# A decoder block with product-key experts on one core: six un-normed query units, six score banks, an earlier decode and a first phase of 88 blocks

## The chip, the core and the metric

The kernel runs on one core of a Trainium2 chip. The metric is the device time of one execution in microseconds (us). The engines are TensorE (PE, with its weight loads PEld), VectorE (DVE), ScalarE (ACT), GpSimd (POOL) and SyncE (SP, which issues DMAs).

## What is computed

One layer on 512 tokens of width 1024, in fp32. Its first half mixes gated linear attention and sliding-window attention. The second half is PEER: each of 8 heads finds, for each token, the 16 best of 16384 experts by two sets of 128 keys, and sums the chosen experts. Cut to what matters here:

```python
h = rmsnorm(x, norm_mix_g); proj = h @ w_in               # GLA and attention branches follow
x = x + (sigmoid(gate_a) * y_a + sigmoid(gate_b) * y_b) @ w_out
xn = rmsnorm(x, norm_ffn_g)
qp = (xn @ w_pq).reshape(t, 8, 2, 128)                    # 16 query units of 128
scores = einsum('thpd,hpkd->thpk', qp, sub_keys)          # 128 keys a side
s_top, i_top = top_k(scores, 16)
cand = s_top[:, :, 0, :, None] + s_top[:, :, 1, None, :]  # 16 x 16, the best 16 of them
best, pos = top_k(cand, 16)
idx = i_top0 * 128 + i_top1                               # at pos
gate = softmax(best)
out = sum_k gate_k * gelu(expert_u[idx_k] . xn) * expert_v[idx_k]
x = x + out
```

## The kernel before

**Precision and weights.** Each fp32 weight unit (128 x 1024) is loaded (raw), cast to fp32r by ACT (whi, line 162) and completed by a subtraction on DVE or POOL (wlo, line 172). A product takes three matmuls: hi by hi, hi by lo, lo by hi (`proj`, line 231; a unit of 128 columns takes 24). The splits run ahead of use through three buffers of each kind, so that a late wlo delays TensorE only after about two units.

**Stages in order.** The mixing half runs to 529.8 us. The gate of the linear attention (`gr`) gets a tanh and a product (`gr_act`, `gr_late`) beside the sliding-window attention, whose products are the matmuls of line 489 on the tile pc.

Then 16 query units (wpq). For unit hp, `proj` makes the queries in PSUM. The first NXU units use the un-normed xuh/xul (x times the norm's weight) and DVE multiplies the result by rb, the reciprocal rms of each token; the others use xh/xl, the normed input, which `xn_hi` and `xn_lo` make (rb itself is ready only after the first unit). `scores(hp)` multiplies queries and keys into a PSUM bank (tag PT or O in turn), `top16` finds the best 16 of 128 on DVE, twice eight, and after two units (one head) `cands` does the same with the head's 72 candidates. `xtok_fill` transposes the normed input of the first tokens back to rows (16 transposes) through the same banks PT and O.

Then all 16384 experts are computed densely for tokens 144 to 511, in 128 blocks of 128: a U block (`h_step`, 24 matmuls into hp, gelu on ACT into ring or hw) and a V block (`v_step`, 24 matmuls into the eight accumulators oacc/oa). They run in three phases: U blocks 0 to N0 - 1, then their V blocks, then the same for the next 20 blocks and for the rest. U results that don't fit the ring go to DRAM (hw to hs, on ACT's queue) and come back during V.

**Beside the first phase** runs the route. The generator `route` decodes positions into expert numbers on DVE, in steps; the table RS says behind which block each step stands. A decoded token group is written into the gate table g by 128 scatters (`scatter`, POOL, line 1143, address tile addr) and by one-hot matmuls (`gmm`, gp). LEAD is the block from which `feed` builds the latter. POOLLO is the number of dense units whose wlo POOL makes. For the first 144 tokens, expert rows are fetched instead (`gather`, POOL, line 1310, 26 early "row" and then "rows" in pairs), with a product and an addition on DVE and a gelu of one column on ACT (lines 1281 and 1282) for each.

**The turns.** Ahead of V, `g_load` brings a slice of the gate table (gt); `w_a` multiplies it by the ring (wr) and casts it (wh), `w_b` makes the rest (wl). Behind V, `sum_phase` copies the accumulators out to yT, so that the next U blocks can use the banks; `pump` issues the next step of the row work where a planner's counters (pe, dve, dma, pool) say that there is room. Each engine runs its instructions in the order in which the code issues them; each DMA queue does as well.

Of the kernel before, what the change touches and what calls it, by code (L numbers as in the profile page):

```python
# [20 lines left out]
D = 1024  # L21
T = 512
NT = 4
# [9 lines left out]
NGA = 6  # L33
NXU = 3
RS = (4, 7, 8, 10, 11, 11, 12, 12, 13, 13, 14, 14, 15, 15, 16, 16, 17, 17, 18, 18, 19, 19, 20, 20, 21, 21, 22, 22)
DVELO = 20
NWARM = 11
POOLLO = 8
DS = (1, 3, 5, 7, 9, 11, 13, 16)
# [7 lines left out]
NB = 128  # L47
N0 = 92
NRP = 10
NOO = 4  # L50
AHEAD = 3
LEAD = 23
TAIL = 5
# [30 lines left out]
def tile_block(ctx, tc, xT, wst, smalls, wgk2, keysT, uT, vv, uv_rows, out):  # L84
# [186 lines left out]
    for kb in range(KB):  # L271
        g = S("gmix")[:, kb:kb + 1]
        nc.scalar.activation(hhi[:, kb], xt[:, kb], AF.Copy, scale=g)
        nc.vector.scalar_tensor_tensor(hlo[:, kb], xt[:, kb], g, hhi[:, kb].bitcast(F32), OP.mult, OP.subtract)
        if kb < 4:
            st.first(kb // 2, kb % 2)
    xs = Bt[:, 0]
    rb = F.tile([128, T], F32, name="rb", tag="rb")
# [332 lines left out]
    for d in range(8):  # L611
        w = unit("gr")
        if d == NR:
            flush()
            gb = F.tile([128, KB, T], F32, name="gb", tag="gb")
            side.append(swa())
            nm[0] = 3
            st.defer = True
        ps = proj(w, H, each=tick)
        nc.vector.tensor_tensor(gr[:, d], ps, rb, OP.mult)  # L620
        gr_late()
        if d >= NR:
            gr_act(d)
            if d < 2 * NR:
                gr_act(d - NR)
    for d in range(8):
# [245 lines left out]
    xtok = XP.tile([128, D], F32, name="xtok")  # L872
    xtk2 = XP.tile([128, D], F32, name="xtk2", tag="xtk2")
    x2d = DR.tile([XP_, D], F32, name="x2d")
    x1s = DR.tile([128, NT, D], F32, name="x1s")
# [47 lines left out]
    nc.scalar.activation(rb, rb, AF.Exp, scale=-0.5)  # L923
    newton(rb, ssq, 1.0 / D, xtok[:, T:])
    nc.scalar.copy(x1t[:, :, 7 * 128:], p)
    nc.sync.dma_start(x1s, x1t)
    xn0 = F.tile([128, KB, 256], F32, name="xn0", tag="gr")
    XN, XU = (xh, xl), (xuh, xul)
    misc = XP.tile([128, 512], F32, name="misc")
    qpt = [xtk2[:, 0:T], xtk2[:, T:], misc[:, 0:T]]  # L930
# [8 lines left out]
    def xn_lo(kb):  # L939
        eng = nc.vector if kb in (1, 3, 6) else nc.gpsimd  # L940
        eng.tensor_tensor(xl[:, kb], hr[kb], xh[:, kb].bitcast(F32), OP.subtract)
        h = hr.pop(kb)
        nc.scalar.copy(xn0[:, kb, 0:128], h[:, 0:128])
        nc.scalar.copy(xn0[:, kb, 128:128 + XP_].rearrange("p (r t) -> p r t", t=XG),
                       h[:, None, 128:TG].to_broadcast([128, XR, XG]))

    def xtok_fill(dst, c, n, hf):
        p = PS.tile([128, 512], F32, name="tp", tag="PT" if hf else "O")
        for i in range(4):
            nc.tensor.transpose(p[0:n, i * 128:(i + 1) * 128], xn0[:, hf * 4 + i, c:c + n], ident)  # L950
        nc.scalar.copy(dst[0:n, hf * 512:(hf + 1) * 512], p[0:n, :])


    vt, it, w1, w2 = slot(name="vals"), slot(U32, "idx"), slot(name="w1"), slot(name="w2")
    vals, idx = [[x[:, i * 512:(i + 1) * 512].rearrange("p (t h k) -> p t h k", t=NT, h=8) for i in range(2)] for x in (vt, it)]
# [5 lines left out]
    def top16(jobs):  # L961
# [8 lines left out]
        for v, ix, src, tmp in jobs:  # L970
            nc.vector.max_index(ix[:, 8:16], v[:, 8:16], tmp)

    def scores(hp):
        qp = qps.pop(hp)
        sc = PS.tile([128, NT, 128], F32, name="sc", tag="PT" if hp % 2 else "O")
        for t in range(NT):
# [15 lines left out]
    for hp in range(17):  # L992
        if hp < 16:
            w = unit("wpq")
            ps = proj(w, XU if hp < NXU else XN)
            if hp == 0:
                xn_hi(0)
            if hp < NXU:
                nc.vector.tensor_tensor(qpt[hp], ps, rb, OP.mult)
            else:  # L1000
                nc.scalar.copy(qpt[hp % 2], ps)
            qps[hp] = qpt[hp if hp < NXU else hp % 2]
            if hp == 0:
                for kb in range(1, KB):
                    xn_hi(kb)
                    xn_lo(kb - 1)
                xn_lo(KB - 1)
        if hp:
            scores(hp - 1)
        if hp % 2 and hp >= 3:  # L1010
            cands((hp - 3) // 2)
        if hp == NXU - 1:
# [5 lines left out]
            R = sR.enter_context(tc.tile_pool(name="route", bufs=1, side="left"))  # L1018
            gate = R.tile([128, NT, 8, 16], F32, name="gate")
            best = gate  # L1020
            idf = R.tile([128, NT, 2, 16, 8], BF, name="idf")
# [178 lines left out]
    def route():  # L1200
# [5 lines left out]
        nc.vector.tensor_tensor(idd[:, :, 1:16], idf[:, :, 0, 1:16], idf[:, :, 0, 0:15], OP.subtract)  # L1206
        yield
        mx = R.tile([128, 32], F32, name="gmax")
        nc.vector.tensor_copy(mx, b32[:, :, 0])
# [58 lines left out]

    late, early, used, acc2 = [False], [0], [-1], []
    nxt, born, end, en = [], {}, [False], [0]  # L1270
    sel = XP.tile([128, XG], F32, name="sel")
# [15 lines left out]
    def gather():  # L1287
# [8 lines left out]
        def issue(k):  # L1296
            nonlocal grp, n
            while n < min(n_, k + (3 if late[0] else 2) + 2 * end[0]):
                for i in range(min(2 if late[0] else 1, n_ - n)):
# [50 lines left out]
        issue(0)  # L1350
        pu, pv = 0, 0
        nxt[:] = [0]
        yield
# [21 lines left out]
    def h_step(b, each=None):  # L1375
        w = get("U", b)
        if b < N0 and b % 2 == 0:
            if b % 4 == 0:
                two[0] = PS.tile([128, 2, 512], F32, name="hp2", tag="S2")
            bank = two[0][:, b % 4 // 2]  # L1380
        else:
            bank = PS.tile([128, 512], F32, name="hp", tag=f"M{(b // 2 if b < N0 else b) % 2}")
        ps = proj(w, XN, n=TD, c0=TG, bank=bank, each=each)
# [94 lines left out]
    def pump():  # L1478
        for x in (dve, dma, pool):
            x[0] = max(x[0], pe[0] - SLACK)  # L1480
        for _ in range(2):
            if side and max(dve[0], dma[0], pool[0] - (0 if late[0] else POOLQ)) < pe[0] + SLACK:
                if nxt and not late[0] and pe[0] < born[nxt[0]] + LAND:
# [42 lines left out]

    BANKS = ("S2", "S2", "PT", "O", "M2", "M3", "M0", "M1")
    b_s = NB
    for ph, (b0, b1) in enumerate(PHASES):
        for b in range(b0, b1):  # L1530
            if b == b1 - 1:
                w_a(b0 // 2)
                w_b(b0 // 2)
                w_a(b0 // 2 + 1)
            h_step(b, feed if LEAD <= b < N0 - GL else None)
            if b == RS[0]:
                dve[0] = 27.0
            for _ in range(RS.count(b)):
                next(r_)
            if b == RS[-1]:  # L1540
                side.append(gather())
            if b == N0 - TAIL - 4:
                late[0] = True
            if b == N0 - TAIL - 1:
# [5 lines left out]
            if b == N0 - GL:  # L1550
# [3 lines left out]
                g_load(0, nc.gpsimd)  # L1554
                g_load(1, nc.gpsimd)
            pool[0] = max(pool[0], pe[0] - SLACK)
            if scs:
# [14 lines left out]
        for b in range(b0, b1 - 2 if last else b1):  # L1572
# [8 lines left out]
            if b % 2 == 0 and p + 1 < b1 // 2:  # L1581
                w_b(p + 1)
            v_step(b, b == b0, b == b1 - 1)
            pump()
            if b == NB - 6:
# [3 lines left out]
                nc.sync.dma_start(xr[:, 2:4], x1s[:, 2:4])  # L1589
        if not last:  # L1590
            sum_phase(ph)
    wl_ = [get("V", NB - 2), get("V", NB - 1)]
# [91 lines left out]
```

## Time and profile before

| | |
|---|---|
| runs | 1754.71, 1765.33, 1756.65 us; median 1756.65 |
| profiled execution | 1764.95 us, of which the span is 1763.0 |
| TensorE granted clock, mean | 0.992 |
| busiest engines | PE 98%, DVE 74%, ACT 43%, POOL 40% |
| DMA | 423.88 MB, 240 GB/s in the mean |

The trace is of one execution. A time of a row is from the span's start. Matmul ends are modelled and overlap, so times of neighbouring starts give the pace.

### The profile page before, as it was taken

The page shows a single profiled execution, that of the slowest core. Times are in us where ns is not written, and L with a number is a line of the kernel's source. Part 1 is how long each engine was busy: PE and PEld are TensorE (multiplying, and loading weights), DVE is VectorE, ACT ScalarE, POOL GpSimd, SP SyncE. Part 2 cuts the span into 40 slices and gives each one's busy share as a digit, 9 for nine tenths or more (in the row PEclk, how much of TensorE's full clock was granted, in tenths as well). Part 3 has the DMA queues.
Part 4 walks back from the last instruction along what each step waited for, and adds up shares of the span by engine and source line. Part 5 has one row for each costly group of instructions (what it writes and reads, how often), then busy time and mean ns, then how long its engine had stood idle before and what let it go on. Part 6 is the DMA issues. An engine that isn't in the chain of part 4 may idle for free.

```text
span 1763.0 us, 26377 instructions
## 1 busy us (share of the span) xinstructions
PE 1724.8 (98%) x9866; PEld 1599.9 (91%) x9866; DVE 1304.9 (74%) x2547; ACT 765.9 (43%) x1334; POOL 705.9 (40%) x447
## 2 busy tenths in 40 slices
PE   9999999999998999999999999999999998999998
PEld 7776688988886889999999989999999998999998
DVE  7767624346337996977778746999889998899874
ACT  5545523335244234355555533444444434444441
POOL 0004444445544451778788872222122223233200
PEclk9999999999998999999999999999999999999999
DMA  4214522222234234699999998999999999999963
GB/s 171 96 60 120 166 98 84 84 72 83 90 129 152 79 104 142 137 267 248 278 290 301 294 304 328 412 412 407 408 404 398 371 386 349 401 377 388 378 244 107
DMA packets 163231, 423.88 MB, mean 240 GB/s; under 512 B 34704, under 2 KB 80144, under 8 KB 144288
## 3 DMA queue, kind: packets, MB, share of 16 engines
q1 hardware_dynamic: 118432, 256.06, 41.9%
q0 software_dynamic: 39488, 152.59, 24.3%
q10 hardware_dynamic: 5184, 13.57, 2.1%
q8 instruction: 77, 1.26, 0.3%
q14 instruction: 50, 0.41, 0.1%
HBM read 379.67 MB, written 42.47 MB: 239 GB/s over the span
## 4 chain that ended last, share of the span: by engine, by line
PE 73%; DMA 8%; DVE 7%; POOL 6%; issue 4%; ACT 2%; SPq 0%; DVEq 0%; POOLq 0%; ACTq 0%
PE oa L1445 21%; PE mm L231 18%; PE hp L231 15%; PE oacc L1445 7%; PE mm L248 6%; POOL g L1143 5%; DMA g<-w,addr 2%; DMA rows<-in_uv_rows_dram,misc 2%; DMA row<-in_uv_rows_dram,misc 2%; DMA gt<-g 1%; POOL row L1310 1%; PE sc L977 1%; PE gp L1188 1%; DVE stt L456 1%; DMA raw<-in_uT_dram 1%
## 5 line engine op out<-in xcount | busy, mean ns | idle before, releaser
L162 ACT CAST whi<-raw 128x1024 fp32r<-128x1024 f32 x347 | 361.6, 1045 | 134.9 <-PE mm L231 26.7
L172 DVE TENSOR_TENSOR wlo<-raw,whi 128x1024 fp32r<-128x1024 f32 x266 | 324.4, 1220 | 58.7 <-ACT whi L162 18.8
L231 PE MATMUL hp<-xh,whi 128*128 128x368 f32 x1024 | 345.1, 337 | 10.2 <-ACT hw L1393 5.7
L1310 POOL DMA_INDIRECT rows<-in_uv_rows_dram,misc x118 | 163.5, 1385 | 454.8 <-DVE accv L1342 381.1
L231 PE MATMUL hp<-xh,wlo 128*128 128x368 f32 x1024 | 339.4, 331 | 0.8 <-DVE wlo L172 0.8
L231 PE MATMUL hp<-xl,whi 128*128 128x368 f32 x1024 | 338.8, 331 | 0.0
L1143 POOL DMA_INDIRECT g<-w,addr x128 | 247.4, 1933 | 95.3 <-issue 43.9
L172 POOL TENSOR_TENSOR wlo<-raw,whi 128x1024 fp32r<-128x1024 f32 x81 | 198.5, 2456 | 156.5 <-ACT whi L162 152.5
L1445 PE MATMUL oa<-wl,whi 128*128 128x368 f32 x768 | 254.0, 331 | 0.0
L1445 PE MATMUL oa<-wh,whi 128*128 128x368 f32 x768 | 253.8, 330 | 0.0
L1445 PE MATMUL oa<-wh,wlo 128*128 128x368 f32 x768 | 253.6, 330 | 0.0
L231 PEld LDWEIGHTS hp<-xh,whi 128*128 128x128 f32 x1024 | 194.1, 190 | 11.9 <-ACT hw L1393 7.1
L231 PEld LDWEIGHTS hp<-xh,wlo 128*128 128x128 f32 x1024 | 193.9, 189 | 1.4 <-DVE wlo L172 1.4
L231 PEld LDWEIGHTS hp<-xl,whi 128*128 128x128 f32 x1024 | 194.2, 190 | 0.0
L1445 PEld LDWEIGHTS oa<-wh,whi 128*128 128x128 f32 x768 | 144.8, 189 | 0.0
L1445 PEld LDWEIGHTS oa<-wh,wlo 128*128 128x128 f32 x768 | 144.8, 189 | 0.0
L1445 PEld LDWEIGHTS oa<-wl,whi 128*128 128x128 f32 x768 | 144.7, 188 | 0.0
L1342 DVE SCALAR_TENSOR_TENSOR accv<-rows,misc,accv 128x1024 f32<-128x1024 f32 x102 | 130.7, 1281 | 15.9 <-ACT misc L1282 15.9
L1325 DVE SCALAR_TENSOR_TENSOR rows<-rows,xtok 128x1024 f32<-128x1024 f32 x102 | 124.6, 1221 | 5.7 <-DMA rows<-in_uv_rows_dram,misc 5.6
L1281 ACT ACTIVATE misc<-misc 128x1 f32<-128x1 f32 x144 | 29.4, 204 | 224.7 <-DVE rows L1325 176.4
L231 PE MATMUL mm<-hhi,whi 128*128 128x512 f32 x256 | 104.1, 406 | 0.0
L231 PE MATMUL mm<-hhi,wlo 128*128 128x512 f32 x256 | 100.0, 391 | 0.0
(593 smaller groups left out, 3300.0 us busy)
## 6 DMA issues: line engine op xcount, KB each, us to landing
raw<-in_uT_dram SPq DMA_DIRECT2D x128, 512.0 KB, 5.2
raw<-in_vv_dram SPq DMA_DIRECT2D x128, 512.0 KB, 8.6
raw<-in_wst_dram SPq DMA_DIRECT2D x92, 512.0 KB, 3.5
gt<-gd SPq DMA_DIRECT2D x30, 480.0 KB, 8.6
gd<-gbuild SPq DMA_DIRECT2D x56, 256.0 KB, 6.7
hs<-hw ACTq DMA_DIRECT2D x36, 368.0 KB, 5.3
ring<-hs SPq DMA_DIRECT2D x36, 368.0 KB
g<-zero SPq DMA_DIRECT2D x16, 512.0 KB, 5.7
```

Of the source, the lines that this page charges most:

```text
L162: nc.scalar.copy(hi, self.raw[u])
L172: self.lo_eng(u).tensor_tensor(lo, r, hi.bitcast(F32), OP.subtract)
L231: nc.tensor.matmul(ps[:, :n], a[:, kb, :], b[:, kb, c0:c0 + n], start=(kb == 0 and i == 0), stop=(kb == KB - 1 and i == 2))
L248: nc.tensor.matmul(banks[t], a[:, kb, t * 128:(t + 1) * 128], b[:, k, :], start=(first and k == 0 and i == 0), stop=(last and k == kk - 1 ...
L456: nc.vector.tensor_reduce(nm, m, AX.X, OP.max, negate=True)
L977: nc.tensor.matmul(sc[:, t], qp[:, t * 128:(t + 1) * 128], ky[hp], start=True, stop=True)
L1143: i = nc.gpsimd.indirect_dma_start(out=g3, out_offset=bass.IndirectOffsetOnAxis(ap=addr[:, c:c + 1], axis=0), in_=w3[:, c:c + 1], in_offse ...
L1281: nc.scalar.activation(h, h, AF.Gelu)
L1310: nc.gpsimd.indirect_dma_start(out=rows[n], out_offset=None, in_=uv_rows, in_offset=bass.IndirectOffsetOnAxis(ap=ix[:, slots[n][1]:slots[n ...
L1325: nc.vector.scalar_tensor_tensor(cur, cur, 1.0, xs_[kind][0:m, :], OP.mult, OP.mult, accum_out=hc)
L1342: nc.vector.scalar_tensor_tensor(a_, cur, h_[0:m, s_:s_ + 1], a_, OP.mult, OP.add)
L1445: nc.tensor.matmul(accs[c][:, 0:TD], v_[:, cs], a, start=(first and i == 0), stop=(last and i == 2))
```

## The change

1. Score stage. NXU goes from 3 to 6. ACT copies the un-normed queries as they are; the scores of the first three heads therefore lack the factor rb, which doesn't alter the order within a token, and `route` multiplies these heads' gates by rtk (rb per token, brought to the partitions by four small matmuls after the second unit). The scores use six banks in turn (PT, O, two halves of S2, M2, M3), the projections and `xtok_fill` the two banks M0 and M1. xn_hi and xn_lo are spread over the first three units, all on DVE; `xtok_fill` and the load of the later keys follow unit 5 instead of unit 2.
2. Decode in blocks 3 to 17 (26 steps) instead of 4 to 22 (28); POOLLO 5 instead of 8; LEAD 18 instead of 23; U blocks ahead of LEAD alternate between two banks.
3. N0 is 88: phases of 88, 20 and 20 blocks.
4. From block 77 on no row is fetched until g_load has been issued (held), and the fetches follow it on POOL.
5. `sum_phase` is issued before the row step behind the last V block, the last two accumulators swap banks, and the first w_a and w_b of phases 1 and 2 stand one block earlier.
6. In the front, the second weight unit is split at kb = 5, and gr_act of the first gates is spread over the later ones.

Its core:

```diff
 NGA = 6
-NXU = 3
-RS = (4, 7, 8, 10, 11, 11, 12, 12, 13, 13, 14, 14, 15, 15, 16, 16, 17, 17, 18, 18, 19, 19, 20, 20, 21, 21, 22, 22)
+NXU = 6
+XNB = {0: (0, 1, 2, 3), 1: (4, 5), 2: (6, 7)}
+RS = (3, 3, 4, 5, 6, 6, 6, 7, 7, 8, 9, 10, 10, 10, 12, 12, 12, 12, 13, 13, 13, 15, 15, 15, 16, 17)
 DVELO = 20
 NWARM = 11
-POOLLO = 8
+POOLLO = 5
 DS = (1, 3, 5, 7, 9, 11, 13, 16)
...
 NB = 128
-N0 = 92
+N0 = 88
 NRP = 10
...
 AHEAD = 3
-LEAD = 23
+LEAD = 18
 TAIL = 5
...
             st.first(kb // 2, kb % 2)
+        elif kb == 5:
+            st.splits(3)
     xs = Bt[:, 0]
...
             gr_act(d)
-            if d < 2 * NR:
-                gr_act(d - NR)
+            if d >= NR + 2:
+                gr_act(d - NR - 2)
     for d in range(8):
...
     xtk2 = XP.tile([128, D], F32, name="xtk2", tag="xtk2")
+    misc = XP.tile([128, 512], F32, name="misc")
     x2d = DR.tile([XP_, D], F32, name="x2d")
...
     nc.scalar.activation(rb, rb, AF.Exp, scale=-0.5)
-    newton(rb, ssq, 1.0 / D, xtok[:, T:])
+    newton(rb, ssq, 1.0 / D, misc)
     nc.scalar.copy(x1t[:, :, 7 * 128:], p)
...
     XN, XU = (xh, xl), (xuh, xul)
-    misc = XP.tile([128, 512], F32, name="misc")
     qpt = [xtk2[:, 0:T], xtk2[:, T:], misc[:, 0:T]]
...
     def xn_lo(kb):
-        eng = nc.vector if kb in (1, 3, 6) else nc.gpsimd
-        eng.tensor_tensor(xl[:, kb], hr[kb], xh[:, kb].bitcast(F32), OP.subtract)
+        nc.vector.tensor_tensor(xl[:, kb], hr[kb], xh[:, kb].bitcast(F32), OP.subtract)
         h = hr.pop(kb)
...
     def xtok_fill(dst, c, n, hf):
-        p = PS.tile([128, 512], F32, name="tp", tag="PT" if hf else "O")
+        p = mbank()
         for i in range(4):
...
+    gate = RA.tile([128, NT, 8, 16], F32, name="gate")
+    best = gate
     vt, it, w1, w2 = slot(name="vals"), slot(U32, "idx"), slot(name="w1"), slot(name="w2")
...
+    sc2 = [None]
+    nm[0] = 2
+
     def scores(hp):
         qp = qps.pop(hp)
-        sc = PS.tile([128, NT, 128], F32, name="sc", tag="PT" if hp % 2 else "O")
+        if hp % 6 // 2 == 1:
+            if hp % 2 == 0:
+                sc2[0] = PS.tile([128, 2, NT, 128], F32, name="sc2", tag="S2")
+            sc = sc2[0][:, hp % 2]
+        else:
+            sc = PS.tile([128, NT, 128], F32, name="sc", tag=("PT", "O", "", "", "M2", "M3")[hp % 6])
         for t in range(NT):
...
             ps = proj(w, XU if hp < NXU else XN)
-            if hp == 0:
-                xn_hi(0)
-            if hp < NXU:
-                nc.vector.tensor_tensor(qpt[hp], ps, rb, OP.mult)
-            else:
-                nc.scalar.copy(qpt[hp % 2], ps)
-            qps[hp] = qpt[hp if hp < NXU else hp % 2]
-            if hp == 0:
-                for kb in range(1, KB):
-                    xn_hi(kb)
+            qps[hp] = qpt[hp % 3 if hp < NXU else hp % 2]
+            nc.scalar.copy(qps[hp], ps)
+            for kb in XNB.get(hp, ()):
+                xn_hi(kb)
+                if kb:
                     xn_lo(kb - 1)
-                xn_lo(KB - 1)
+                if kb == KB - 1:
+                    xn_lo(kb)
         if hp:
             scores(hp - 1)
+        if hp == 1:
+            ps = mbank()
+            for t in range(NT):
+                nc.tensor.matmul(ps[:, t:t + 1], rb[0:1, t * 128:(t + 1) * 128], ones[0:1, 0:1], start=True, stop=True)
+            rtk = RA.tile([128, NT], F32, name="rtk")
+            nc.scalar.copy(rtk, ps[:, 0:NT])
         if hp % 2 and hp >= 3:
...
             R = sR.enter_context(tc.tile_pool(name="route", bufs=1, side="left"))
-            gate = R.tile([128, NT, 8, 16], F32, name="gate")
-            best = gate
             idf = R.tile([128, NT, 2, 16, 8], BF, name="idf")
...
         yield
+        un = gate[:, :, 0:NXU // 2]
+        nc.vector.tensor_tensor(un, un, rtk[:, :, None, None].to_broadcast([128, NT, NXU // 2, 16]), OP.mult)
         mx = R.tile([128, 32], F32, name="gmax")
...
     late, early, used, acc2 = [False], [0], [-1], []
+    held, more = [False], []
     nxt, born, end, en = [], {}, [False], [0]
...
             nonlocal grp, n
-            while n < min(n_, k + (3 if late[0] else 2) + 2 * end[0]):
+            while not held[0] and n < min(n_, k + (3 if late[0] else 2) + 2 * end[0]):
                 for i in range(min(2 if late[0] else 1, n_ - n)):
...
         pu, pv = 0, 0
+        more.append(lambda: issue(pv))
         nxt[:] = [0]
...
         w = get("U", b)
-        if b < N0 and b % 2 == 0:
-            if b % 4 == 0:
+        if LEAD <= b < N0 and b % 2 == 0:
+            if b % 4 == 0 or two[0] is None:
                 two[0] = PS.tile([128, 2, 512], F32, name="hp2", tag="S2")
...
         else:
-            bank = PS.tile([128, 512], F32, name="hp", tag=f"M{(b // 2 if b < N0 else b) % 2}")
+            bank = PS.tile([128, 512], F32, name="hp", tag=f"M{(b // 2 if LEAD <= b < N0 else b) % 2}")
         ps = proj(w, XN, n=TD, c0=TG, bank=bank, each=each)
...
         for _ in range(2):
-            if side and max(dve[0], dma[0], pool[0] - (0 if late[0] else POOLQ)) < pe[0] + SLACK:
+            if side and (early[0] or not held[0]) and max(dve[0], dma[0], pool[0] - (0 if late[0] else POOLQ)) < pe[0] + SLACK:
                 if nxt and not late[0] and pe[0] < born[nxt[0]] + LAND:
...
-    BANKS = ("S2", "S2", "PT", "O", "M2", "M3", "M0", "M1")
+    BANKS = ("S2", "S2", "PT", "O", "M2", "M3", "M1", "M0")
     b_s = NB
...
         for b in range(b0, b1):
-            if b == b1 - 1:
+            if b == b1 - (2 if ph else 1):
                 w_a(b0 // 2)
                 w_b(b0 // 2)
+            if b == b1 - 1:
                 w_a(b0 // 2 + 1)
...
             if b == RS[0]:
-                dve[0] = 27.0
+                dve[0] = 15.0
             for _ in range(RS.count(b)):
...
                 side.append(gather())
-            if b == N0 - TAIL - 4:
-                late[0] = True
+            if b == N0 - TAIL - 6:
+                late[0] = held[0] = True
             if b == N0 - TAIL - 1:
...
                 g_load(1, nc.gpsimd)
+                held[0] = False
+                more[0]()
             pool[0] = max(pool[0], pe[0] - SLACK)
...
             v_step(b, b == b0, b == b1 - 1)
+            if b == b1 - 1 and not last:
+                sum_phase(ph)
             pump()
...
                 nc.sync.dma_start(xr[:, 2:4], x1s[:, 2:4])
-        if not last:
-            sum_phase(ph)
     wl_ = [get("V", NB - 2), get("V", NB - 1)]
...
     for c in range(7, -1, -1):
```

How instructions stand on the engines at three places (each row: line, operation, out<-in, size, how many in a row; the lines of the changed kernel are a few higher).

TensorE at the end of the third query unit (mm is the unit's bank, sc a score bank, tp the bank of a transposition). Before, the scores of unit 1 are followed by the sixteen transposes and then by the first unit on normed input:

```order
L231 MATMUL mm_4439<-xuh,whi_4306 128x512
L231 MATMUL mm_4439<-xul,whi_4306 128x512
L231 MATMUL mm_4439<-xuh,wlo_4308 128x512
L977 MATMUL sc<-xtok,xtk_3939 128x128 x4
L950 MATMUL tp<-ident,xn_4298 128x128 x16
L231 MATMUL mm_4539<-xh,whi_4378 128x512
L231 MATMUL mm_4539<-xl,whi_4378 128x512
L231 MATMUL mm_4539<-xh,wlo_4380 128x512
```

In the changed kernel these rows stand at the end of the sixth unit, and the transposes go into four projection banks (mm) one after the other:

```order
L232 MATMUL mm_4648<-xuh,whi_4507 128x512
L232 MATMUL mm_4648<-xul,whi_4507 128x512
L232 MATMUL mm_4648<-xuh,wlo_4509 128x512
L989 MATMUL sc<-xtok,xtk_3939 128x128 x4
L952 MATMUL mm_4719<-ident,xn_4302 128x128 x4
L952 MATMUL mm_4725<-ident,xn_4302 128x128 x4
L952 MATMUL mm_4731<-ident,xn_4302 128x128 x4
L952 MATMUL mm_4737<-ident,xn_4302 128x128 x4
L232 MATMUL mm_4763<-xh,whi_4584 128x512
L232 MATMUL mm_4763<-xl,whi_4584 128x512
L232 MATMUL mm_4763<-xh,wlo_4586 128x512
```

The transposes have moved three units back and out of the score banks.

POOL ahead of the V blocks of phase 0 (g is the gate table, gd and g the sources of gt, rows the expert rows). Before:

```order
L1143 DMA g_79<-w_5498,addr 2097152x1 x6
L1310 DMA rows<-in_uv_rows_dram,misc 128x2048 x4
L1410 DMA gt<-gd 128x960
L1411 DMA gt<-g_79 128x512
L1410 DMA gt<-gd 128x960
L1411 DMA gt<-g_79 128x512
L1310 DMA rows<-in_uv_rows_dram,misc 128x2048 x114
```

And in the changed kernel:

```order
L1155 DMA g_79<-w_5505,addr 2097152x1 x6
L1426 DMA gt<-gd 128x960
L1427 DMA gt<-g_79 128x512
L1426 DMA gt<-gd 128x960
L1427 DMA gt<-g_79 128x512
L1325 DMA rows<-in_uv_rows_dram,misc 128x2048 x118
```

Four fetches of rows have moved from ahead of the loads of gt to behind them.

ACT at the end of phase 0's V blocks (whi the casts of weights, misc the one-column gelu and its scaling, yT the copies out of the accumulators oa, ring the first gelu of the next U blocks). Before:

```order
L162 CAST whi_13467<-raw_13432 128x1024
L1281 ACTIVATE misc<-misc 128x1
L1282 ACTIVATE misc<-misc 128x1
L1502 COPY yT<-oa 128x368 x2
L162 CAST whi_13502<-raw_13469 128x1024
L1393 ACTIVATE ring<-hp 128x368
```

And in the changed kernel:

```order
L163 CAST whi_13161<-raw_13129 128x1024
L163 CAST whi_13195<-raw_13163 128x1024
L1518 COPY yT<-oa 128x368 x2
L1296 ACTIVATE misc<-misc 128x1
L1297 ACTIVATE misc<-misc 128x1
L163 CAST whi_13230<-raw_13197 128x1024
L1409 ACTIVATE ring<-hp 128x368
```

The copies have moved ahead of the one-column gelu.

## The prediction

> **What bounds the kernel now.** I read the page's first lines, then TensorE's waits, then the stretches around the longest waits. All times are us.
>
> ```profile
> span 1763.0 us, 26377 instructions
> PE 1724.8 (98%) x9866; PEld 1599.9 (91%) x9866; DVE 1304.9 (74%) x2547; ACT 765.9 (43%) x1334; POOL 705.9 (40%) x447
> ```
>
> TensorE is the bound: 38 us of the span are without a matmul. A change that leaves the matmuls alone, as this one nearly does, can win only from these 38 and from time at a lowered clock. Where they are, TensorE's waits say (us in all, times, the longest):
>
> ```profile
> PE hp L231 <- ACT hw L1393: 5.7, 4, 3.0
> PE tp L950 <- DVE w L967: 5.2, 2, 4.2
> PE hp L231 <- ACT yT L1502: 4.5, 1, 4.5
> PE oacc L1445 <- ACT wh L1429: 3.5, 2, 3.1
> PE sc L977 <- DVE xtk L999: 2.1, 1, 2.1
> PE mm L248 <- DVE wlo L172: 1.6, 1, 1.6
> PE o__1251 L489 <- DVE pc L475: 1.4, 1, 1.4
> PE o__1137 L489 <- DVE pc L475: 1.4, 1, 1.4
> PE sc L977 <- ACT qb L1001: 1.4, 1, 1.4
> PE o__1197 L489 <- DVE pc L475: 1.3, 1, 1.3
> PE warm L202 <- DVE eps L104: 1.1, 1, 1.1
> PE oacc L1445 <- DVE wl L1435: 1.0, 2, 0.5
> PE hp L231 <- DVE wlo L172: 0.8, 1, 0.8
> ```
>
> Four places matter: the score stage (tp and both sc rows, 8.7 together), the turn from U to V blocks in phase 0 (oacc, 3.1 + 0.5), the turn from V back to U (yT, 4.5), and the spills (hw, 5.7). The change touches the first three.
>
> **Front part.** The second weight unit is split two steps earlier: the wait of 1.6 (mm <- wlo) can go. I take -1.2, between 0 and -1.6. In the attention stage the spread tanh and products should shorten the three waits on pc (1.4, 1.4, 1.3 = 4.1): less work of other kinds stands ahead of pc on DVE, but pc still needs its own chain. I take -1.8, between 0 and -2.4.
>
> **Score stage.** The stretch from the first query projection to the first U block, then a slow piece of it, then the cadence of later units (columns: length, busy time of PE, PEld, DVE, ACT, POOL, the granted clock):
>
> ```profile
> 529.77:647.50 117.73, 109.07 (x532) 91.52 (x531) 105.40 (x658) 37.43 (x63) 51.63 (x52) 0.94 0.32 111
> 550.00:552.00 2.00, 1.80 (x8) 1.51 (x8) 2.00 (x16) 1.81 (x2) 1.54 (x2) 0.50 0.00 0
> ```
> ```profile
> 570.08 5.46 PE mm L231 x24
> 576.44 5.47 PE mm L231 x24
> ```
> ```profile
> 558.07 2.88 PE L950 MATMUL tp<-ident,xn 128*128 128x128 f32 x12 [4.25 <-DVE w L967]
> ```
>
> A unit with its four score matmuls takes 576.44 - 570.08 = 6.36; sixteen take 101.8. The sixteen transposes of xtok come to 1.9 at full clock (twelve took 2.88 at about half). The floor is 103.7. Before, 117.73 - 109.07 = 8.66 were idle and 109.07 - 103.7 = 5.4 went to the lowered clock behind the gaps. The gaps come from one knot: the transposes need the banks PT and O that the scores hold until DVE's top 16 has read them, and DVE is then behind with rms, xn_hi and xn_lo. With six score banks and projection banks for the transposes, no bank waits for DVE there; with six un-normed units TensorE needs xn only from unit 6, 38 us after the start, and DVE loses three multiplications. It gains five xn_lo that POOL had: two operations of 128x512 more, at most 1.2 each by the wlo row below (128x1024), inside the 10.37 that DVE now waits (quoted with it below). The scaling of three heads' gates by rtk is one more such operation in the decode. What is late next: four transposed halves share two banks, so two wait for an ACT copy of about 0.5 each (+1.0); the keys from 5 on are loaded after the fills (I take again the 1.4 of the qb row; between 0, when unit 6 covers the load, and 4); the four tiny matmuls for rtk with their copy cost +0.3, which the next unit's projection may hide. New length 103.7 + 1.0 + 1.4 + 0.3 = 106.4, so **-11.3**, between -8 and -13.
>
> [...] After a wait of 2.1 the clock was 0.50 in the piece above. [...]
>
> **DVE from there on.** How full DVE is while the scores run out, and in the decode that follows:
>
> ```profile
> 570.10:666.40 96.30, 96.30 (x507) 84.72 (x507) 96.16 (x708) 27.34 (x35) 49.27 (x54) 1.00 0.30 96
> 666.40:734.40 68.00, 68.00 (x409) 67.97 (x409) 53.27 (x85) 30.04 (x43) 26.35 (x15) 1.00 0.50 133
> ```
> ```profile
> 570.12 0.89 DVE L963 MAX8 vals<-sc 128x8 f32<-128x128 f32 x4 [10.37 <-PE sc L977]
> ```
> ```profile
> L172 DVE TENSOR_TENSOR wlo<-raw,whi 128x1024 fp32r<-128x1024 f32 x17 | 20.7, 1220 | 9.4 <-PE hp L231 9.4
> ```
>
> Before, DVE waited 10.37 for scores at 570 and was then busy to 666.4, 18.9 behind the first U block (647.5). Without that wait it ends near 655, again 18.8 behind the new first block (529.8 + 106.4 = 636.2). Behind it the decode is now squeezed: its steps cost DVE about 40 (53.27 less 20.7 for wlo is 32.6 in these seventeen blocks of 4.00, 68.00 / 17; the remaining steps of the schedule bring it to 40, an estimate), and fifteen blocks bring fifteen wlo of 1.22 less overlap, 17. So 57 of work stand between 655 and the end of block 17 at 708; three wlo buffers let DVE be two blocks (8) late, to 716. It fits with 4 to spare. ACT must follow too:
>
> ```profile
> 667.96 2.38 ACT L1204 CAST idf<-idx 128x256 bf16<-128x256 uint32 x4
> ...
> 680.14 1.28 ACT L1211 ACT_TABLE_LOAD   x1
> 681.43 0.63 ACT L1211 ACTIVATE gate<-gate 128x512 f32<-128x512 f32 x1
> ```
>
> These 2.38, 0.63 and two table loads of 1.28 now fall together in blocks 3 to 4, ahead of a gelu that frees one of only two U banks (block LEAD on has four). Going through the blocks by hand I find block 6 0.75 late and block 13 0.3 late: **+1**, between 0 and +10.
>
> [...]
>
> **U to V in phase 0.** The chain on POOL decides when the gate table is complete (columns: busy us, mean ns, idle before):
>
> ```profile
> L1143 POOL DMA_INDIRECT g<-w,addr x128 | 247.4, 1933 | 95.3 <-issue 43.9 <-DVE addr L1138 36.5 <-DMA g<-w,addr 13.8
> L1310 POOL DMA_INDIRECT row<-in_uv_rows_dram,misc x26 | 36.2, 1392 | 7.9 <-issue 6.7 <-DVE wlo L172 0.6 <-DVE oh L1175 0.6
> ```
> ```profile
> 706.79 2.45 POOL L1143 DMA_INDIRECT g<-w,addr  x1 [36.50 <-DVE addr L1138]
> ```
> ```profile
> 1064.32 18.18 DMA gt<-g
> ```
> ```profile
> 1083.92 0.44 PE L1445 MATMUL oacc<-wh,whi 128*128 128x368 f32 x1 [3.14 <-ACT wh L1429]
> ```
> ```profile
> 1084.00:1088.00 4.00, 3.48 (x13) 3.23 (x14) 4.00 (x6) 2.13 (x3) 0.00 (x0) 0.69 0.26 62
> 1088.00:1092.00 4.00, 4.00 (x23) 4.00 (x22) 3.15 (x6) 1.14 (x5) 0.00 (x0) 0.88 0.87 299
> ```
>
> From the first scatter POOL needs 247.4 + 36.2 + (95.3 - 36.5) + 7.9 = 350, to 1057. Then four gathers for two later rows stood ahead of the load of gt (7 more); it took 18.2 to land, and 1.4 later V began, after 3.14 + 0.52 of waiting and with 4 x 0.31 + 4 x 0.12 = 1.7 lost to the clock. After: addr is ready near 677 (the front's -3 included), the scatters end near 1027, nothing stands ahead of the load, which issues at 1028 and lands at 1047; V could start at 1049. TensorE ends its 88 U blocks at 1051 (before 647.5 to 1080.8 for 92; four blocks of 4.0 fewer; all shifted by -3.0 - 11.3 + 1). So the wait goes: **-4.5** of 5.4, between 0 and -5.4. What is held: no row is fetched from block 77 to 82, and DVE's row products queue behind that; DVE has them to make up later, beside V, where it is not the bound. The four U and V blocks that move from phase 0 to phase 2 cost there what they cost here; two spills fewer.
>
> **V back to U.** ACT's queue at that turn, and the clock after it:
>
> ```profile
> 1458.76 0.20 ACT L1281 ACTIVATE misc<-misc 128x1 f32<-128x1 f32 x1 [3.16 <-DVE rows L1325]
> ...
> 1459.20 0.81 ACT L1502 COPY yT<-oa 128x368 f32<-128x368 f32 x2
> ```
> ```profile
> 1460.00:1464.00 4.00, 3.94 (x13) 3.94 (x14) 2.30 (x3) 0.96 (x2) 0.00 (x0) 0.50 1.02 415
> 1464.00:1468.00 4.00, 4.00 (x25) 4.00 (x24) 1.23 (x1) 1.63 (x6) 0.00 (x0) 0.95 0.63 253
> ```
>
> The copies that free the first U banks stood behind a gelu that waited 3.16 for a row on DVE. Issued before the row's step, they start at 1455.6, as TensorE ends: the wait falls from 4.5 to about 0.6, and the clock loss, 4 x 0.50 + 4 x 0.05 = 2.2, with it: **-6.1**, between -3 and -6.7. The gelu now waits behind the copies, 0.8, and delays a row only. Preparing the first pair one block earlier in phases 1 and 2 takes the two short waits (0.5 on wl, 0.4 of the 3.5 on wh): -0.9.
>
> **Sum.** -1.2 - 1.8 - 11.3 + 1 - 4.5 - 6.1 - 0.9 = -24.8. Against the profiled execution's own 1764.95 that is 1740.2; the median of the runs shown is 1756.65, 8.3 less, and if that difference lies in parts that the change leaves alone, the time is 1731.9. I predict the middle, **1736**.
>
> **Rivals.**
> 1. DVE doesn't keep up in blocks 3 to 17 (chance 0.18): DVE busy 57 of 61 leaves no room for steps that run slower beside POOL, and every us past the two blocks of slack stops TensorE. For it: the 0.8 (hp <- wlo) that waits even now. About 10 of the gain is given back: 1744 to 1755. That the score stage doesn't do what it says, since top 16 on DVE and not the banks sets its pace, ends there too: DVE's 96.16 of 96.30 speaks for it, but TensorE lost nothing in that stretch, which speaks against.
> 2. The spill waits (5.7 and their clock) shrink as well, since fewer row transfers run beside the last spills (0.14): 1723 to 1728.
> 3. Slower (0.08): the scatter chain doesn't move with its start. Its 350 hold 58.8 of idle time, 13.8 on scatters before, and may stretch beside gathers that now start at block 17. Behind the start of V stand 1764.95 - 1083.92 = 681, plus four U blocks (16), less 7.0: 690. At 1049 plus a stretch the time goes 1 for 1; from a chain of 376 (V at 1075) it is slower than before, from about 394 by over 1%. Against it: the scatters' pace came from POOL's own 1933 ns each, not from waits.
>
> **The numbers.** Forecast 0.60 (1728 to 1744), rivals as above. Range 1724 to 1754: it leaves out the tail of rival 2 and rival 3. One per cent (1739.1, 1774.2) is about what a measurement of this kernel can tell from no change: the lower two thirds of the forecast and rival 2 are faster, 0.54; rival 3 is slower beyond it with 0.05; the rest 0.41.
>
> **What would show it.** Right: no row of tp or sc over 1.5 in TensorE's waits, granted clock 1.00 in the score stage, first U block 106 after the first query projection; first scatter 27 to 30 earlier; no wait of oacc on wh, V at about 1050; yT wait under 1. Wrong: waits of hp on wlo in blocks 5 to 19 (rival 1), a load of gt that lands after the last U block (rival 3).

## The result, and the profile after

The changed kernel takes 1749.66 us (median of 20 runs, 1740.19 to 1759.63), the kernel before 1758.73 (20 runs, 1748.69 to 1771.98). The ratio is 0.9947 with a 95% interval of 0.9924 to 0.9970: 9 us faster. The prediction had -24.8 as its sum and 1736 as its time.

The first lines of the changed kernel's page, and TensorE's three longest groups of waits in it (us in all, times, the longest):

```profile
span 1745.6 us, 26366 instructions
PE 1719.7 (99%) x9874; PEld 1594.8 (91%) x9874; DVE 1308.1 (75%) x2553; ACT 765.9 (44%) x1338; POOL 692.5 (40%) x439
```
```profile
PE sc L989 <- DVE w L971: 4.2, 1, 4.2
PE hp L232 <- ACT hw L1409: 2.9, 3, 1.6
PE sc L989 <- DMA raw<-in_wst_dram: 1.8, 1, 1.8
```

The rows of tp, of oacc on wh and of yT are gone. A new one leads: the scores wait for DVE once, for 4.2. The places of the prediction follow, in its order.

**Score stage.** The stage and the piece behind it (columns as in the prediction), then TensorE's and DVE's rows at its end:

```profile
528.38:642.93 114.55, 107.37 (x539) 90.02 (x538) 109.77 (x695) 40.72 (x68) 48.74 (x59) 0.99 0.34 115
641.00:647.00 6.00, 5.76 (x21) 5.80 (x22) 6.00 (x49) 0.00 (x0) 3.60 (x8) 0.50 0.41 117
```
```profile
636.01 1.06 PE L989 MATMUL sc<-qb 128*128 128x128 f32 x8
641.24 2.04 PE L989 MATMUL sc<-qb 128*128 128x128 f32 x8 [4.17 <-DVE w L971]
```
```profile
640.80 0.29 DVE L971 MATCH_REPLACE8 w<-vals,sc 128x128 f32<-128x128 f32 x1
```

The stage took 114.55 instead of 106.4. The scores of unit 14 are done at 637; those of unit 15 start at 641.24, just after DVE has read the last of unit 14's. The clock is then at 0.50 into the first U block.

**U to V.** First and last scatter, and the first load of gt:

```profile
687.27 2.45 POOL L1155 DMA_INDIRECT g<-w,addr  x1 [31.59 <-DVE addr L1150]
```
```profile
1028.02 1.54 POOL L1155 DMA_INDIRECT g<-w,addr  x1 [0.31 <-issue]
1034.13 0.61 POOL L1426 DMA_DIRECT2D gt<-gd  x1 [4.57 <-DMA gd<-gbuild]
```

From the first scatter to the end of the last, the chain took 342 (forecast 350; the three profiles of the kernel before have 350, 337 and 347), from a start 19.5 earlier. The loads of gt waited 4.57 for gd and issued at 1034 instead of 1028. But they took only 7.7, 8.8 and 10.2 to land (the three of four whose landing the trace has; 18.2 and 19.6 before) and so landed by 1046, forecast 1047. V began at 1056.6 without a wait.

**V to U.** ACT's copies out of the accumulators, and the first matmul behind them, with no idle time ahead of it:

```profile
1410.64 0.82 ACT L1518 COPY yT<-oa 128x368 f32<-128x368 f32 x2
```
```profile
1412.60 0.33 PE L232 MATMUL hp<-xh,whi 128*128 128x368 f32 x1
```

### The profile page after: what moved, and what is told of

Same layout as the page of the kernel before. It is cut to its first block, busy times and chain, and to the rows that moved or that the text cites. A ratio compares the mean times of both kernels' runs of the same rounds, so it can differ in the third digit from the quotient of the medians.

```text
span 1745.6 us, 26366 instructions
## 1 busy us (share of the span) xinstructions
PE 1719.7 (99%) x9874; PEld 1594.8 (91%) x9874; DVE 1308.1 (75%) x2553; ACT 765.9 (44%) x1338; POOL 692.5 (40%) x439
## 4 chain that ended last, share of the span: by engine, by line
PE 63%; DVE 13%; DMA 10%; POOL 6%; issue 5%; ACT 3%; SPq 1%; DVEq 0%; ACTq 0%; POOLq 0%
PE oa L1461 16%; PE mm L232 16%; PE hp L232 13%; PE mm L249 6%; PE oacc L1461 5%; POOL g L1155 5%; DMA raw<-in_vv_dram 4%; DVE wlo L173 2%; DMA rows<-in_uv_rows_dram,misc 2%; DMA g<-w,addr 2%; PE gp L1200 1%; DMA raw<-in_uT_dram 1%; DMA row<-in_uv_rows_dram,misc 1%; DVE rows L1340 1%; DVE w L971 1%
## 5 line engine op out<-in xcount | busy, mean ns | idle before, releaser
L173 POOL TENSOR_TENSOR wlo<-raw,whi 128x1024 fp32r<-128x1024 f32 x78 | 191.9, 2464 | 160.7 <-ACT whi L163 151.3
```

What stands on the lines that cost most here:

```text
L173: self.lo_eng(u).tensor_tensor(lo, r, hi.bitcast(F32), OP.subtract)
```

## The experiments

Each experiment was timed beside fresh runs of the kernel before, whose medians went from 1752.0 to 1760.7; its ratio is to these runs, and need not be that of the two medians. Medians of two experiments that differ by a few us are therefore compared with care, and by their ratios where it matters.

To compare profiles I split each by the starts of the first matmuls of its stages. Within a column the work is the same, except that phases of 88 blocks (the last three rows) move four U and four V blocks, 16.1 for each four, into the last column (lengths in us):

| profile | front | score stage | U, phase 0 | V, phase 0 | rest | span |
|---|---|---|---|---|---|---|
| before | 529.8 | 117.5 | 436.6 | 376.2 | 302.9 | 1763.0 |
| before_again | 530.2 | 116.7 | 424.2 | 375.3 | 302.3 | 1748.7 |
| before_look3 | 530.2 | 116.2 | 432.6 | 373.9 | 302.7 | 1755.6 |
| after | 528.4 | 114.5 | 413.7 | 356.0 | 333.0 | 1745.6 |
| after_sc15 | 528.8 | 108.8 | 417.9 | 353.0 | 334.3 | 1742.8 |
| sc15_land20 | 528.7 | 108.5 | 407.5 | 356.4 | 337.2 | 1738.3 |

### Is the wait at the end of the score stage a false one? (after_sc15)

```diff
-        if hp % 6 // 2 == 1:
+        if hp % 6 // 2 == 1 and hp < 15:
...
-            sc = PS.tile([128, NT, 128], F32, name="sc", tag=("PT", "O", "", "", "M2", "M3")[hp % 6])
+            sc = PS.tile([128, NT, 128], F32, name="sc", tag=("PT", "O", "", "M2", "M2", "M3")[hp % 6])
```

> The changed kernel, but the scores of unit 15 go into bank M2 instead of the second half of the double bank S2. Theory A (the 4.2 us that TensorE waits there, and the half clock behind it, come from the two halves being one tile: the write of the second half waits until DVE has read the first half's scores of unit 14): the 4.2 wait goes, the first U block starts 4 to 5 us earlier (score stage 110 instead of 114.6), another 1.5 to 2 from the clock, together 5 to 7 us under the changed kernel. Rival (TensorE waits for DVE's top 16 of an earlier unit in any bank, as DVE is about one unit behind): a wait of 3 to 4 stays at the same place, time unchanged.

It took 1740.68 us, a ratio to before of 0.9903 (0.9869 to 0.9938). Its score stage, the longest wait left in it, and TensorE around the four small matmuls for rtk:

```profile
528.80:637.60 108.80, 106.39 (x537) 89.09 (x536) 104.56 (x660) 38.45 (x67) 44.13 (x47) 1.00 0.35 119
```
```profile
PE sc L989 <- DMA raw<-in_wst_dram: 1.2, 1, 1.2
```
```profile
541.00 1.05 PE L1021 MATMUL mm<-ones,rb 1*128 1x1 f32 x8
542.75 0.50 PE L232 MATMUL mm<-xuh,whi 128*128 128x512 f32 x1 [0.70 <-ACT xtk L1009]
```

The wait and the half clock are gone: 5.7 in the stage. The two halves of the double bank were one tile, and only at the end does no projection stand between the two units that share it. The rival falls. Labels below that begin with sc15 have this edit too.

### How much of the first profile was one execution's luck? (before_again, before_look3)

> The kernel before, unchanged, profiled a second time. Theory A (the first profile was of a slow execution: its stalls at the turn from V to U, at the turn from U to V and at the spills are longer than usual): a span some 4 to 12 us below 1763.0, the difference found in these waits (14.1 together in the first profile) and in the clock behind them, the score stage (117.7) the same within 1. Theory B (the difference between executions is spread evenly or lies in the mixing half): the same three waits within 2 us, the difference elsewhere.

> The kernel before, unchanged, timed and profiled a third time. The stretch from the first U block of phase 0 to its first V block took 436.6 and 424.2 us in two profiles. Theory A (stalls behind late DMAs in this stretch come and go): again between 424 and 437, and what it has over 424 is the sum of TensorE's waits on hw, wh, wl and wlo there and of the lowered clock behind them, within 1.5; the shorter executions have the higher granted clock. Rival (the stretch itself runs at another pace): more than 3 us over 424 that no wait and no lowered clock accounts for.

The unchanged kernel took 1750.6 in the one run of before_again, and 1757.34 in before_look3, with a ratio of 1.0003 (0.9969 to 1.0038) to itself. TensorE's waits in the U blocks of phase 0 and at the turn, in the two:

```profile
PE hp L231 <- DVE wlo L172: 0.4, 1, 0.4
```
```profile
PE hp L231 <- ACT hw L1393: 5.5, 4, 1.9
PE hp L231 <- ACT misc L1282: 1.8, 1, 1.8
PE oacc L1445 <- DVE wl L1435: 0.2, 1, 0.2
```

The turn from U to V, worth 3.66 and 1.7 of clock in the first profile, waited 0 and 0.2 here. U of phase 0 less its waits and the lowered clock is 425.3, 423.8 and 425.4 in the three profiles: all but 1.6 of the difference between executions is these stalls. The wait on yT is in each (4.5, 6.1, 4.1). So theory A of before_again holds for the turn from U to V and for the spills, not for the turn from V to U.

### What are the stalls of phase 0? (sc15_hw3, sc15_land20, rs92_land20, b_land20)

First, three spill buffers instead of two, paid with one ring buffer:

```diff
-NRP = 10
+NRP = 9
...
-                ring[p] = Dn.tile([128, 2, TD], F32, name="hw", tag="hw", bufs=2)
+                ring[p] = Dn.tile([128, 2, TD], F32, name="hw", tag="hw", bufs=3)
```

> The changed kernel with unit 15's scores in M2, and three spill buffers hw instead of two, paid with one ring buffer less (NRP 9, one spill more). Theory A (U blocks wait for a spill's transfer to free its buffer, 3 to 6 us in most profiles): no wait of hp on hw over 0.5, 3 to 5 us shorter, and a narrower spread of runs. Rival (the gelu that frees hp is late for another reason, such as ACT's queue holding a transfer's issue): waits of 2 to 5 stay, time the same within 2.

It took 1742.19, 0.9923 (0.9895 to 0.9951), not less than after_sc15 with 1740.68 (0.9903): theory A falls. A wait of 1.5 on hw stays, and one of 3.6 on wlo is there. Behind the latter, on TensorE, DVE and ACT:

```profile
817.64 0.44 PE L232 MATMUL hp<-xh,wlo 128*128 128x368 f32 x1 [3.56 <-DVE wlo L173]
```
```profile
815.21 1.22 DVE L1340 SCALAR_TENSOR_TENSOR row<-row,xtok 128x1024 f32<-128x1024 f32 x1 [8.05 <-DMA row<-in_uv_rows_dram,misc]
...
816.36 1.22 DVE L173 TENSOR_TENSOR wlo<-raw,whi 128x1024 fp32r<-128x1024 f32 x1
```
```profile
816.48 0.20 ACT L1296 ACTIVATE misc<-misc 128x1 f32<-128x1 f32 x1 [7.50 <-DVE row L1340]
816.71 0.29 ACT L1297 ACTIVATE misc<-misc 128x1 f32<-128x1 f32 x1
816.91 0.46 ACT L1409 ACTIVATE hw<-hp 128x368 f32<-128x368 f32 x1
```

DVE stood 8 us at a row that had not landed; wlo and, on ACT, the block's gelu stood behind it. The new theory: late rows, not full spill buffers. The planner counts a row as landed LAND us after its fetch, while the early rows of the first profile took 6.5 to 11.8 (median 9.1, of those whose landing it has); the next runs double LAND.

```diff
-LAND = 10.0
+LAND = 20.0
```

> The changed kernel with unit 15's scores in M2, and the planner's LAND at 20 instead of 10: a fetched row's product is issued 20 us and not 10 after its fetch, in the planner's time. Theory A (the stalls of U blocks in phase 0, listed under hw and wlo, are DVE waiting up to 8 us at the head of its queue for a row that has not landed, with ACT's one-column gelu and then the block's gelu behind it): DVE's waits for row in phase 0 fall from 67 us to under 30, no wait of a U block over 1, U blocks of phase 0 take 412 instead of 418, 3 to 6 us shorter in all. Rival (the stalls come from full spill buffers or late weights): the waits of hp stay at 3 to 6.

> The same with decode schedule and phases of before (92 blocks), LAND 20. Theory A: as with 88 blocks, 0 to 4 us shorter than with LAND 10 (whose profile shows 2.8 of waits on hw). Rival: the later products push the row work into the V blocks or past the turn, where a wait of 2 to 4 appears; time the same or longer.

> The kernel before with LAND 20 alone. Theory A: its U blocks of phase 0 take 424 to 427 where three profiles showed 424, 433 and 437; 4 to 8 us shorter in the median, with fewer runs above 1755. Rival (spill transfers or late weights): no change.

sc15_land20 took 1737.38, 0.9899 (0.9869 to 0.9929); its six runs go from 1735.6 to 1740.1, the twelve of after_sc15 from 1733.8 to 1756.6. With 92 blocks and the decode schedule of before (rs92_land20) it is 1738.50, 0.9907 (0.9876 to 0.9937). The kernel before with LAND 20 alone took 1749.14, 0.9977 (0.9954 to 1.0000), with no run above 1753.5 where the runs beside it reach 1768.9. None of the three has a wait of TensorE in these U blocks. DVE's row products there (idle time ahead of them at the end), in before, before_again, before_look3 and sc15_land20:

```profile
L1325 DVE SCALAR_TENSOR_TENSOR row<-row,xtok 128x1024 f32<-128x1024 f32 x26 | 31.8, 1224 | 62.2 <-DMA row<-in_uv_rows_dram,misc 62.1
```
```profile
L1325 DVE SCALAR_TENSOR_TENSOR row<-row,xtok 128x1024 f32<-128x1024 f32 x26 | 31.7, 1219 | 34.4 <-DMA row<-in_uv_rows_dram,misc 34.4
```
```profile
L1325 DVE SCALAR_TENSOR_TENSOR row<-row,xtok 128x1024 f32<-128x1024 f32 x26 | 31.7, 1221 | 64.3 <-DMA row<-in_uv_rows_dram,misc 53.6 <-issue 10.7
```
```profile
L1340 DVE SCALAR_TENSOR_TENSOR row<-row,xtok 128x1024 f32<-128x1024 f32 x18 | 21.9, 1216 | 0.0
```

The shortest execution of before is the one in which DVE waited least for rows. So it is shown that the stalls are late rows (but for the longest of before, 2.99 at 1054.91, ahead of which a weight took 9.61 to land), and that later products remove them. The 8 early rows fewer are not the reason: b_land20 has 18 as well, and its U blocks take 423.5, as in before_again without its wait (423.8). What it is worth in the whole is less sure: the long runs are gone, but sc15_land20 is not told apart from after_sc15 by its ratio, and the interval of b_land20 reaches 1.0000. In rs92_land20 a wait of 3.7 on yT stands at the turn from V to U, as its rival said, and the form is not shorter than sc15_rs92 below (0.9901).

### The turn from V to U (b_sum, sc15_sumlate)

```diff
             v_step(b, b == b0, b == b1 - 1)
+            if b == b1 - 1 and not last:
+                sum_phase(ph)
             pump()
...
-        if not last:
-            sum_phase(ph)
```

> The kernel before with only the order at the end of V blocks changed: sum_phase is issued ahead of the row step. Theory A (the stall of 4.5 us and 2.2 us of clock seen at that turn is present in each execution): 6 us shorter. Rival (it is present only in some executions, where a row lands late, and usually shorter): 0 to 3 us shorter in the median.

> The changed kernel with unit 15's scores in M2, and sum_phase again behind the row step (the rest of the change kept). Theory A (issuing the copies ahead of the row step removed the wait of yT, 4.5 and 6.1 us in two profiles of before, and the clock behind it): a wait of 4 to 6 on yT comes back at the turn from V to U, 6 to 8 us longer than the same kernel with sum_phase first. Rival (the swapped banks and the earlier w_a, or the row's luck, removed it): wait under 2, time the same within 2.

b_sum took 1753.35, 0.9936 (0.9903 to 0.9969). The wait on yT fell to 0.8 in its profile, but another came at the next turn, and before it, on DVE, a late row:

```profile
PE oacc L1445 <- ACT wh L1429: 4.9, 1, 4.9
```
```profile
1526.78 1.23 DVE L1325 SCALAR_TENSOR_TENSOR rows<-rows,xtok 128x1024 f32<-128x1024 f32 x1 [3.26 <-DMA rows<-in_uv_rows_dram,misc]
```

This form lacks the w_a that the change issues a block earlier, which would have stood ahead of that row. sc15_sumlate (the order undone in after_sc15) took 1744.67, 0.9935 (0.9905 to 0.9966), 4 longer than after_sc15 by the medians, with 2.5 of wait on yT: between the two theories. So the order is worth about 4 when it is undone, and when it is added alone 6 by the medians (1759.20 beside it) and 5 to 17 by the interval of the ratio: it pays, and the 6.1 of the sum is neither confirmed nor refuted.

The order removes one cause of this wait, not the wait. With it kept, yT is still waited for in sc15_land20 (2.0), rs92_land20 (3.7) and sc15_noheld (4.5). In sc15_land20 the copies stood behind the cast of a weight that landed late:

```profile
1399.64 1.04 ACT L163 CAST whi<-raw 128x1024 fp32r<-128x1024 f32 x1 [2.41 <-DMA raw<-in_uT_dram]
1400.59 0.83 ACT L1518 COPY yT<-oa 128x368 f32<-128x368 f32 x2
```

### Decode schedule and phases (sc15_rs92)

The edit puts RS, LEAD 23, POOLLO 8, N0 92 and dve[0] = 27 back in after_sc15.

> The changed kernel with unit 15's scores in M2, and decode schedule, LEAD, POOLLO and phases of before (92, 20, 16); held fetches, order of the turns, score stage and front stay changed. Theory A (early decode and 88 blocks cancel: the gate table is wanted 16 us sooner and is ready 20 us sooner, and a U block costs the same in either phase): the same time within 3 us, wait at the turn from U to V under 2. Rival (the earlier decode is part of the gain): a wait of 2 to 4 at that turn with its half clock, 3 to 6 us longer.

It took 1738.48, 0.9901 (0.9871 to 0.9930), with no wait at the turn from U to V: theory A. The earlier decode only pays for the earlier turn: without either, after_sc15 gains as much.

### The hold (sc15_noheld, sc15_late6, b_held)

```diff
-            if b == N0 - TAIL - 6:
-                late[0] = held[0] = True
+            if b == N0 - TAIL - 4:
+                late[0] = True
...
-                held[0] = False
-                more[0]()
```

sc15_late6 keeps N0 - TAIL - 6 for the switch; b_held has the hold alone in the kernel before.

> The changed kernel with unit 15's scores in M2, with rows fetched ahead of g_load again (late from four blocks before the end of the row buffers, no hold). Theory A (with 88 blocks the loads of gt have some 4 us to spare, and four fetches of 1.4 to 2.0 us stand ahead of them): a wait of 1 to 4 at the turn from U to V, with half clock if it is over 2; 0 to 5 us longer. Rival (the hold is idle): no wait there, same time.

> The changed kernel with unit 15's scores in M2, without the hold only: the switch to paired rows stays at block 77, 26 early rows as in the changed kernel, but four fetches of rows stand ahead of the loads of gt on POOL. Theory A (these four fetches are what costs: gt lands 5 to 7 us later, V starts late, the first pairs of the V blocks are late too): a wait of 2 to 4 on wh at the turn from U to V, 8 to 18 us longer than with the hold. Rival (the 18 us that the form without hold and with the later switch cost came from the switch two blocks later, with a 27th early row in the way): at most 5 us longer.

> The kernel before with the hold alone (switch at block 81 instead of 83, no fetch until the loads of gt are issued). Theory A (the hold is worth something by itself): no wait on wh at the turn from U to V, 5 to 12 us shorter. Rival (it only pays for the 16 us that 88 blocks take away): 0 to 3 us shorter.

sc15_noheld took 1758.85, 1.0011 (0.9983 to 1.0039); sc15_late6 1748.34, 0.9949 (0.9920 to 0.9977); b_held 1754.05, 0.9970 (0.9942 to 0.9998). At the turn from U to V sc15_late6 shows these waits, and one of its loads of gt this landing (start, length):

```profile
PE oacc L1461 <- ACT wh L1445: 4.6, 1, 4.6
PE oacc L1461 <- DVE wl L1451: 0.3, 1, 0.3
```
```profile
1039.51 16.90 DMA gt<-gd
```

With 1.7 for a half clock behind it (an estimate, from the 1.7 behind the same turn in the first profile) this 4.9 is most of the 8 that it is longer than after_sc15: the four fetches cost that. They delay the loads of gt by 2.5 to 5, and above all this load then takes 17 to land, where those of the changed kernel took 8 to 10. The expectation of sc15_noheld had 0 to 5 and missed. Its other 10 come with the switch two blocks later and its 27th early row. In its profile they lie behind the turn, in V (360.2 for 355.6 in sc15_late6, with the 4.5 on yT) and in the rest (338.6 for 331.8); why they come is open. Alone in the kernel before the hold gives 5, with an interval that ends near nothing, between the theories.

### The score stage alone (b_score)

The score stage of the change, with U blocks ahead of LEAD on M0 and M1, in the kernel before.

> The kernel before with the score stage of the change alone (six un-normed units, six score banks, spread xn, later transposes, U blocks ahead of block 23 on M0 and M1); decode schedule, phases, turns and front as before. Theory A (the score stage won little by itself, since the false wait of 4.2 us at its end took most of it): 3 us shorter to the first U block, less 2 for the clock behind it, so -1 to -3 of the whole. Rival (the stage alone is the gain of 9 us measured): -7 to -10.

It took 1749.56, 0.9957 (0.9927 to 0.9988). Its profile has the 4.2 wait too and a stage 3 shorter, as theory A says, but its middle of -7.6 is the rival's, and the interval, -2 to -13, does not tell the two apart.

## Why the prediction was wrong

**Score stage, the step that failed most.** "With six score banks ... no bank waits for DVE there" fails for unit 15. The sum had -11.3 with a length of 106.4. Its scores go into the second half of a tile whose first half DVE was still reading, and waited 4.17 for that. Measured: 114.5 after a mean of 116.8 in three profiles of before, and 2 of half clock carried into the first U block, so almost nothing. With the false wait gone it is 108.8, and -8 is what the stage is then worth. Of the 2.4 still missing, 1.5 are the four small matmuls for rtk: with the wait behind them they took 1.75 (541.00 to 542.75), where the sum had 0.3. The keys were sized well (1.2 for 1.4). Rival 1 had named DVE as the pace of the stage and put it off with a stretch of before in which TensorE lost nothing; that stretch had other banks. But DVE is not the pace either: in after_sc15 no row of TensorE waits for it in this stage.

**U to V, mis-sized.** The wait went, as forecast, but partly by luck: the chain on POOL took 342 for 350 from a first scatter at 687, not 677 (680 in after_sc15, without the late score stage), and the loads issued 6 late; that they then landed in 8 to 10 instead of 18 was not in the sum, and it made up for this. And the 5.4 that could be won stood in one of three profiles of before, so a mean of some 2 was there to win. The hold, which the sum put in with this term without a price, is worth about 8 with 88 blocks, and 5 (0 to 10) alone with 92. That the 16 us which 88 blocks take away make the difference is argued, not shown.

**V to U.** -6.1 and -0.9 forecast; V and rest together are 5 shorter in the profiles (376.2, 375.3, 373.9 and 302.6 before; 356.0 + 16.1 and 333.0 - 32.2 after). Right in kind; undone, the new order costs 4 by the medians. The sum took the gelu for the only thing ahead of the copies.

**Front.** -1.7 of -3.0: the weight split gave its 1.6 (its row is gone); the waits on pc did not shrink but spread: 4.1 in the three longest rows before, and 5.4 with the two that the prediction left out (0.7 and 0.6); after, 1.4 + 1.0 + 0.9 + 0.9 + 0.7 + 0.7 in six.

**Decode squeeze.** Right: of the U blocks of phase 0 only the 2.9 on hw waited after, none of it before block 48, so neither the squeezed steps nor the two table loads of 1.28 (at 664.03 and 666.92) reached TensorE. ACT's exponential starts 1.30 after its table load (664.03 to 665.33), and the load 0.02 after the copy ahead of it.

**The own time.** The profile of before was of a long execution. Its U blocks of phase 0 and the wait that ends them hold 9.7 of waits and 1.7 of lowered clock, where the two later profiles hold 0.4 and 7.3 of waits and no lowered clock. Against mean stages of three profiles of before, the change has -1.7 - 2.3 - 1.3 - 3.0 - 1.8 = -10.1 (front, score stage, U, V, rest), near the measured -9.1. The time lies inside the range, but the gain was sized at more than twice what came. The time also lies in rival 1's 1744 to 1755, and that is chance: its mechanism, waits of hp on wlo in the decode, has no row in the changed kernel.

The shortest version here, shorter than the kernel before and the changed one, is sc15_land20, at 0.9899 (0.9869 to 0.9929) of before; after_sc15 without LAND 20 (0.9903) and sc15_rs92 (0.9901) are not told apart from it by their ratios.

## What to carry to other kernels

Where banks are added so that a consumer may lag, check that each is a tile of its own: here two halves of one tile made the second producer wait 4.17 for the first one's consumer. Before a stall of one profile enters a sum, look whether a second profile of the same kernel has it: here the stalls of the U blocks of phase 0 came and went (6.5, 0.4 and 7.3 of waits), and the wait on yT was in all three (4.5, 6.1 and 4.1). Where an order of instructions is changed to end a wait, look at everything that stands ahead, not only at the instruction that one profile shows waiting. Where an engine runs in order, a product of fetched data issued too early stalls everything behind it: here DVE stood 8.05 at a row, wlo on DVE and the block's gelu on ACT stood behind it, and TensorE waited 3.56. What TensorE's wait names (hw, wlo) may be two queues away from its cause (a row).

## What the runs showed of the hardware

The lowered clock doesn't follow the length of a wait alone. Around the wait of 3.56 in sc15_hw3 it stayed at 1.00, behind one of 3.23 in after_sc15 it fell:

```profile
814.00:822.00 8.00, 4.44 (x29) 4.37 (x29) 6.79 (x12) 3.23 (x7) 6.90 (x4) 1.00 0.78 198
```
```profile
862.00:868.00 6.00, 5.94 (x29) 5.94 (x30) 6.00 (x12) 3.18 (x7) 5.08 (x4) 0.72 0.81 136
```

6 x 0.28 is 1.7, as at the turn in the first profile, and 1.7 lost at half clock is a stretch of 3.4: behind the wait in after_sc15 (matmul at 862.06) the matmuls of 128x368 start 0.31 apart from 863.12 to 865.26, and 0.17 apart from 862.33 to 862.83 and from 866.80 on. Such a stretch also followed a wait of 2.05 in after_sc15 (matmul at 999.29; starts again 0.17 apart from 1002.88). So in these traces a wait of 2 to 4 had a price of either nothing (the 3.56) or about 1.7 on top, where the prediction took the loss of the one profile as certain. What decides between the two, no run here shows.
